# Three product kinds of a by-token matmul: interleaved per weight row block, or grouped by kind

## The chip, the core and the metric

The kernel runs on one core of a Trainium2 chip. The metric is the device time of one execution in microseconds (us), the median of three timed runs: 1079.44 us for the kernel before (1079.11 to 1079.62). TensorE is called PE below, VectorE DVE, ScalarE ACT, GpSimd POOL, and the engine that issues the weight transfers SP.

## The reference

Two layers of an encoder trunk over 256 tokens of width 1024, in fp32. Each layer is a gated feed-forward block, a mixer and a second feed-forward block, each added to its input; a norm follows the last layer. Cut to the places that matter here:

```python
x = x + 0.5 * swiglu(rmsnorm(x, ffn1_norm[l]), ffn1_w_gate[l], ffn1_w_up[l], ffn1_w_down[l])
h = rmsnorm(x, mix_norm[l])
z = h @ w_in            # [pool 512 | q 512 | f 512 | i 512 | out-gate 512 | branch gates 2 x 1024]
pool_out = causal_pool_mixer(u_pool, pool_w, pool_scale)
hgrn_out = hgrn2(q, f, i) * silu(og)
g = sigmoid(gates)
merged = g[:, :, 0] * (pool_out @ w_pool_proj) + g[:, :, 1] * (hgrn_out @ w_hgrn_proj)
x = x + merged @ w_out
x = x + 0.5 * swiglu(rmsnorm(x, ffn2_norm[l]), ffn2_w_gate[l], ffn2_w_up[l], ffn2_w_down[l])
```

## The kernel before

**Products in parts.** Weights and activations are fp32, the products use fp32r operands. Each operand is cut into a high part (rounded to fp32r) and a low part (what the rounding left), and a product is the sum of high x high, high x low and low x high. Weights come from HBM in chunks of 128 x 2048 values by SP's queue, in the order of the list `stream`. `parts` (lines 127 to 129) makes a chunk's two parts in two halves of 1024 columns each: ACT casts `raw` to `hi` (L128), DVE subtracts `raw - hi` into `lo` (L129). There are four `raw` buffers and three each of `hi` and `lo`; `weights(key)` prepares three chunks ahead.

**Two shapes of product.** Where the output is wanted with features on partitions, the weights are stationary and the tokens stream: `wide_run` (L182) multiplies 128 x 128 of `hi` with the high and low parts of 256 tokens side by side (512 columns, L186), for all tiles of a chunk, and then 128 x 128 of `lo` with the high parts (256 columns, L188). `mm_wide` (L176) does the same with the two kinds alternating (L179, L180). Where the output is wanted with tokens on partitions, `by_tokens` (L208) has 128 tokens of x stationary, and 512 columns of the weights stream. It is used for v, the out-gate and the four gate blocks of each layer's mixer (x is `xs`), for the two projections `pp` and `hp` of each half b of the 1024 columns, and in `last` for the down projection of the last feed-forward block. A chunk holds four blocks of 128 weight rows, so one call of `by_tokens` on a chunk makes, for each half h of the tokens, four times three products into one PSUM tile (two chunks together in the last group of `last`).

**The end of a mixer, called the merge below.** For b = 0 and 1: `pp` products, times a sigmoid on DVE (L751); `hp` products, times another on DVE (L757) into z, and the sum of both (L758). z is 128 tokens x 512 columns; it has two buffers, and there are four z per layer, named (b, h) below. `turned` (L705) turns each by four PE transposes (L709) into one of two PSUM tiles `gps`, from which ACT takes the high part (L247) and DVE the low part (L248) into the tiles `mhl` (named b4 to b7 in the trace of the first layer). Then the output projection `wo` (chunks 60 to 62 of the first layer) multiplies these by `mm_wide`: its first product needs b4 with the tokens of both halves, so z(0,0) and z(0,1) turned.

**What sets the order.** Tile code is recorded in the order of the source; a scheduler that estimates times then fixes one order of instructions per engine and the buffers. Work inside `urgent()` (z, the transposes, `residual`) gets a higher priority. On the chip each engine goes through its own list in that order, and waits on semaphores where it needs another's result.

Of the kernel before, what the change touches and what calls it, by code (L numbers as in the profile page):

```python
# [68 lines left out]
def _body(ctx, tc, a, out):  # L69
# [9 lines left out]
    mm = nc.tensor.matmul  # L79
# [128 lines left out]
    def by_tokens(pss, ws, x, ks, nk):  # L208


        for h in range(2):
            th = slice(h * P, h * P + P)
            for i, k in enumerate(ks):
                wh, wl = ws[i // 4]
                sl = slice(i % 4 * 512, i % 4 * 512 + 512)
                mm(pss[h], x(k)[:, 0, th], wh[:, sl], start=k == 0, stop=False)  # L216
                mm(pss[h], x(k)[:, 0, th], wl[:, sl], start=False, stop=False)  # L217
                mm(pss[h], x(k)[:, 1, th], wh[:, sl], start=False, stop=k == nk - 1)  # L218

    def urgent():  # L220
        return tc.high_priority(offset=URGENT)
# [136 lines left out]
    def last(hidden):  # L358

        ss = const.tile([P, 2, 2], F32, name="ss")  # L360
        r = const.tile([P, 2, 2], F32, name="ssr")
        for b in range(2):
            cols = slice(512 * b, 512 * b + 512)
            pss = token_tiles()
            for group in ((0,), (1,), (2,), (3,), (4, 5)):
                ws = [weights(("dt", b, i)) for i in group]
                by_tokens(pss, ws, hidden, range(4 * group[0], min(4 * group[-1] + 4, KF)), KF)
            for h in range(2):
                x = fin[1 + h][:, cols]
                with urgent():  # L370
                    nc.vector.scalar_tensor_tensor(
                        out=x, in0=pss[h], scalar=0.5, in1=x, op0=ALU.mult, op1=ALU.add)
                    junk = tmp.tile([P, 512], F32, tag="s1", name="junk")
                    nc.scalar.activation(junk, x, AF.Square, scale=D ** -0.5, accum_out=ss[:, h, b:b + 1])
                    if b == 0:
                        nc.vector.tensor_scalar_add(out=r[:, h, 0:1], in0=ss[:, h, 0:1], scalar1=EPS)
                        nc.gpsimd.tensor_mul(out=x, in0=x, in1=fin[0][:, cols])
                        continue
                    rh = r[:, h, 1:2]
                    tt(out=rh, in0=ss[:, h, 1:2], in1=r[:, h, 0:1], op=ALU.add)  # L380
                    nc.gpsimd.tensor_tensor(out=rh, in0=rh, in1=cst[:, C_M05:C_M05 + 1], op=ALU.pow)
                    first = fin[1 + h][:, 0:512]
                    nc.scalar.mul(out=first, in_=first, mul=rh)
                    nc.scalar.dma_start(out=out[:, h, 0:512], in_=first)
                    nc.vector.scalar_tensor_tensor(
                        out=x, in0=x, scalar=rh, in1=fin[0][:, cols], op0=ALU.mult, op1=ALU.mult)
                    nc.sync.dma_start(out=out[:, h, cols], in_=x)
# [92 lines left out]
    def mixer(l, sq, gain):  # L480
# [31 lines left out]
        for i in range(2):  # L512
            by_tokens(vps, [weights(("v", l, i))], xs, range(4 * i, 4 * i + 4), KD)
# [146 lines left out]
        def token_step(name, i):  # L660
            if i == 0:
                blocks_[name] = token_tiles()
            by_tokens(blocks_[name], [weights((name, l, i))], xs, range(4 * i, 4 * i + 4), KD)
            return blocks_[name]
# [178 lines left out]
```

## Time and profile before

| | us |
|---|---|
| median of three runs | 1079.44 |
| the profiled execution, its own time | 1079.82 |
| its span, first to last instruction | 1078.0 |
| PE busy in the span | 1064.3 (99%) |
| DVE busy | 813.9 (75%) |
| ACT busy | 566.7 (53%) |
| POOL busy | 129.9 (12%) |
| mean granted TensorE clock, of full | 0.998 |

The profiled execution took 1.8 us more than its span, and 0.4 us more than the median. PE's busy time is a sum of modelled spans that overlap; how long PE really needs for a product is read from the distance of one start to the next. PEld is PE's load of the stationary operand, beside the products. In the views below, an idle time in brackets stands with the engine and tile whose result ended it; an instruction of ACT or DVE that has no bracket followed the one before it directly.

### The profile page before, as it was taken

Reading aid. Unit: us, or ns where it says so; the run is one execution under the profiler, and the core shown is the slowest. Engines: PE = TensorE matmul, PEld = TensorE weight load, DVE = VectorE, ACT = ScalarE, POOL = GpSimd, SP = SyncE. Lnnn points to the kernel's source line nnn. Section 1 sums busy time; section 2 is a strip of 40 time slices with the busy share of each in tenths; the row PEclk is TensorE's granted clock in tenths of the full one; section 3 lists DMA queues with packets and bytes.
Section 4 is the critical chain, followed back from the end, with each engine's and each line's share of the span. In section 5 each row is a group of like instructions: output and inputs, shape, how many; then the busy total and the mean of one; then the engine's idle time right before and its main releaser. Section 6 shows DMA issues by size and latency. Waiting matters only on the chain.

```text
span 1078.0 us, 15379 instructions
## 1 busy us (share of the span) xinstructions
PE 1064.3 (99%) x5890; PEld 918.3 (85%) x5890; DVE 813.9 (75%) x1261; ACT 566.7 (53%) x953; POOL 129.9 (12%) x130
## 2 busy tenths in 40 slices
PE   9999999999999999999999999999999999999997
PEld 7888888887888888888888888888878788888885
DVE  7887767789667987777777776777995779777642
ACT  7675544544435655554455555446345456555532
POOL 2000001038100200000100000111560011000010
PEclk9999999999999999999999999999999999999999
DMA  9755456553543655546755544674445446555441
GB/s 332 273 185 174 135 185 232 189 193 116 205 156 121 237 190 194 171 139 189 249 200 192 193 157 140 210 265 169 152 130 183 161 172 234 188 174 191 171 137 39
DMA packets 32506, 197.34 MB, mean 183 GB/s; under 512 B 3616, under 2 KB 4512, under 8 KB 14000
## 3 DMA queue, kind: packets, MB, share of 16 engines
q1 hardware_dynamic: 31824, 195.50, 52.9%
q8 instruction: 46, 0.75, 0.3%
q10 hardware_dynamic: 576, 0.79, 0.2%
q14 instruction: 28, 0.23, 0.1%
q0 software_dynamic: 32, 0.07, 0.0%
HBM read 195.29 MB, written 1.05 MB: 182 GB/s over the span
## 4 chain that ended last, share of the span: by engine, by line
PE 90%; DVE 4%; POOL 3%; issue 2%; DMA 1%; ACT 0%; POOLq 0%; SPq 0%; DVEq 0%
PE ps L186 43%; PE ps L188 22%; PE ps L218 6%; PE ps L217 6%; PE ps L216 6%; PE ps L179 4%; PE ps L180 2%; DVE lo L129 2%; POOL win L636 1%; POOL b L557 1%; POOL b L556 1%; PE gps L590 1%; DMA xg<-in_x 0%; DVE m L555 0%; PE gps L693 0%
## 5 line engine op out<-in xcount | busy, mean ns | idle before, releaser
L129 DVE TENSOR_TENSOR lo<-raw,hi 128x1024 fp32r<-128x1024 f32 (+4 forms) x406 | 461.6, 1172 | 167.8 <-ACT hi L128 128.1
L128 ACT CAST hi<-raw 128x1024 fp32r<-128x1024 f32 (+4 forms) x406 | 373.7, 967 | 276.9 <-PE ps L186 97.7
L186 PE MATMUL ps<-xs__93,hi 128*128 128x512 f32 x1504 | 363.6, 393 | 0.0
L186 PEld LDWEIGHTS ps<-xs__93,hi 128*128 128x128 f32 x1504 | 275.0, 188 | 54.1
L188 PEld LDWEIGHTS ps<-xs__93,lo 128*128 128x128 f32 x1504 | 188.7, 188 | 8.2
L188 PE MATMUL ps<-xs__93,lo 128*128 128x256 f32 x1504 | 191.1, 278 | 0.0
L186 PE MATMUL ps<-b,hi 128*128 128x512 f32 x528 | 128.7, 391 | 0.0
L186 PEld LDWEIGHTS ps<-b,hi 128*128 128x128 f32 x528 | 95.7, 188 | 17.8
L273 POOL TENSOR_TENSOR acc<-acc,sq 128x256 f32<-128x256 f32 x42 | 37.4, 890 | 606.6 <-issue 392.2
L247 ACT CAST b<-h 128x256 fp32r<-128x256 f32 x88 | 35.6, 407 | 131.1 <-DVE h L427 131.1
L217 PE MATMUL ps<-lo,xs__93 128*128 128x512 f32 x192 | 76.9, 400 | 0.0
L216 PE MATMUL ps<-hi,xs__93 128*128 128x512 f32 x192 | 76.7, 399 | 0.0
L218 PE MATMUL ps<-hi,xs__93 128*128 128x512 f32 x192 | 76.2, 397 | 0.0
L202 DVE TENSOR_TENSOR z<-ps,zl 128x256 f32<-128x256 f32 x200 | 75.2, 416 | 0.1
L188 PEld LDWEIGHTS ps<-b,lo 128*128 128x128 f32 x528 | 68.2, 188 | 4.0
L188 PE MATMUL ps<-b,lo 128*128 128x256 f32 x528 | 69.2, 278 | 0.0
L201 ACT COPY zl<-ps 128x256 f32<-128x256 f32 x200 | 63.9, 365 | 6.9 <-PE ps L188 4.2
L423 DVE TENSOR_TENSOR z<-z,rb 128x512 f32<-128x512 f32 x88 | 60.0, 685 | 0.0
L217 PE MATMUL ps<-lo,b 128*128 128x512 f32 x152 | 59.9, 394 | 0.0
L216 PE MATMUL ps<-hi,b 128*128 128x512 f32 x152 | 59.8, 397 | 0.0
L218 PE MATMUL ps<-hi,b 128*128 128x512 f32 x152 | 59.5, 396 | 0.0
L179 PE MATMUL ps<-b,hi 128*128 128x512 f32 x128 | 45.5, 398 | 0.7 <-DVE b L248 0.7
(135 smaller groups left out, 960.6 us busy)
## 6 DMA issues: line engine op xcount, KB each, us to landing
raw<-in_gu SPq DMA_DIRECT2D x82, 1024.0 KB, 4.9
raw<-in_dn SPq DMA_DIRECT2D x48, 704.0 KB, 4.1
raw<-in_wt SPq DMA_DIRECT2D x24, 1024.0 KB, 4.9
raw<-in_wi SPq DMA_DIRECT2D x12, 1024.0 KB, 4.9
raw<-in_dt SPq DMA_DIRECT2D x10, 1024.0 KB, 5.0
raw<-in_wo SPq DMA_DIRECT2D x8, 1024.0 KB, 4.9
raw<-in_gu SPq DMA_DIRECT2D x8, 512.0 KB, 8.4
raw<-in_pp SPq DMA_DIRECT2D x4, 1024.0 KB, 4.9
```

The costliest lines, as they stand in the source:

```text
L128: a = nc.scalar.copy(out=hi[:, sl], in_=raw[:, sl])
L129: return a, tt(out=lo[:, sl], in0=raw[:, sl], in1=hi[:, sl].bitcast(F32), op=ALU.subtract)
L179: mm(ps, wh[:, sl], x, start=start, stop=False)
L186: mm(ps, wh[:, c:c + P], x, start=start, stop=False)
L188: mm(ps[:, 0], wl[:, c:c + P], x[:, 0], start=False, stop=stop)
L201: nc.scalar.copy(out=zl[:, g], in_=pss[g][:, 1])
L202: tt(out=z[:, g], in0=pss[g][:, 0], in1=zl[:, g], op=ALU.add)
L216: mm(pss[h], x(k)[:, 0, th], wh[:, sl], start=k == 0, stop=False)
L217: mm(pss[h], x(k)[:, 0, th], wl[:, sl], start=False, stop=False)
L218: mm(pss[h], x(k)[:, 1, th], wh[:, sl], start=False, stop=k == nk - 1)
L273: return nc.gpsimd.tensor_add(out=self.acc, in0=self.acc, in1=sq)
L423: tt(out=z, in0=z, in1=bc(rb, 2), op=ALU.mult)
```

## The change

Only `by_tokens` is changed. The loop over the three kinds of product now stands outside the loop over the weight row blocks: for a half of the tokens, first all products of x's high part with the weights' high part, then all of x's high part with the weights' low part, then all of x's low part with the weights' high part. Number, shapes, operands and PSUM tile of the products are the same, as are first and last product of each accumulation over a whole width of x. All three kinds now stand on line 216, and every later line number is one less than before.

```diff
         for h in range(2):
             th = slice(h * P, h * P + P)
-            for i, k in enumerate(ks):
-                wh, wl = ws[i // 4]
-                sl = slice(i % 4 * 512, i % 4 * 512 + 512)
-                mm(pss[h], x(k)[:, 0, th], wh[:, sl], start=k == 0, stop=False)
-                mm(pss[h], x(k)[:, 0, th], wl[:, sl], start=False, stop=False)
-                mm(pss[h], x(k)[:, 1, th], wh[:, sl], start=False, stop=k == nk - 1)
+            for part, low in ((0, False), (0, True), (1, False)):
+                for i, k in enumerate(ks):
+                    sl = slice(i % 4 * 512, i % 4 * 512 + 512)
+                    mm(pss[h], x(k)[:, part, th], ws[i // 4][low][:, sl], start=k == 0 and not (part or low),
+                       stop=k == nk - 1 and part == 1)
```

PE, the first out-gate chunk of the first layer (`hi46`, `lo46`; ps_2435 is the half h = 0 of the tokens, ps_2436 h = 1), before:

```order
L216 MATMUL ps_2435<-hi46_2300,xs__93 128x512
L217 MATMUL ps_2435<-lo46_2301,xs__93 128x512
L218 MATMUL ps_2435<-hi46_2300,xs__93 128x512
L216 MATMUL ps_2435<-hi46_2300,xs__93 128x512
L217 MATMUL ps_2435<-lo46_2301,xs__93 128x512
L218 MATMUL ps_2435<-hi46_2300,xs__93 128x512
```

The same place now:

```order
L216 MATMUL ps_2435<-hi46_2300,xs__93 128x512 x4
L216 MATMUL ps_2435<-lo46_2301,xs__93 128x512 x4
L216 MATMUL ps_2435<-hi46_2300,xs__93 128x512 x4
L216 MATMUL ps_2436<-hi46_2300,xs__93 128x512 x4
L216 MATMUL ps_2436<-lo46_2301,xs__93 128x512 x4
L216 MATMUL ps_2436<-hi46_2300,xs__93 128x512
```

What alternated product by product now comes in blocks of four, and the first product with the low part is the fifth and no longer the second.

PE, the merge of the first layer, from the middle of the last `hp` products (ps_3098 is b = 1, h = 1; z_3049 is z(0,1), z_3131 is z(1,0), z_3143 is z(1,1)) to the first `wo` products, before:

```order
L709 MATMUL gps_3052<-cst_91,z_3049 128x128 x4
L216 MATMUL ps_3098<-hi59_3006,b3_2800 128x512
L217 MATMUL ps_3098<-lo59_3007,b3_2800 128x512
L218 MATMUL ps_3098<-hi59_3006,b3_2800 128x512
L216 MATMUL ps_3098<-hi59_3006,b3_2800 128x512
L217 MATMUL ps_3098<-lo59_3007,b3_2800 128x512
L218 MATMUL ps_3098<-hi59_3006,b3_2800 128x512
L179 MATMUL ps_3172<-b4_2963,hi60_3064 128x512
L180 MATMUL ps_3172<-b4_2963,lo60_3065 128x256
```

and further down on PE before, after eight pairs of `wo` products:

```order
L179 MATMUL ps_3274<-b4_2963,hi62_3157 128x512
L709 MATMUL gps_3134<-cst_91,z_3131 128x128 x4
L180 MATMUL ps_3274<-b4_2963,lo62_3158 128x256
L179 MATMUL ps_3274<-b4_2963,hi62_3157 128x512
L180 MATMUL ps_3274<-b4_2963,lo62_3158 128x256
L709 MATMUL gps_3146<-cst_91,z_3143 128x128 x4
L179 MATMUL ps_3172<-b5_2964,hi60_3064 128x512
```

PE there now:

```order
L216 MATMUL ps_3098<-hi59_3006,b2_2799 128x512 x2
L216 MATMUL ps_3098<-hi59_3006,b3_2800 128x512 x2
L708 MATMUL gps_3052<-cst_91,z_3049 128x128 x4
L708 MATMUL gps_3134<-cst_91,z_3131 128x128 x4
L179 MATMUL ps_3172<-b4_2963,hi60_3064 128x512
L180 MATMUL ps_3172<-b4_2963,lo60_3065 128x256
```

The transposes of z(0,1) have moved from within the last `hp` products to behind them, and those of z(1,0) from within the `wo` products to ahead of them. Those of z(1,1) (gps_3146) stay behind ten pairs of `wo` products on b4.

DVE at the same place (`lo62` is the third `wo` chunk; b4_2963<-gps_3052 is the low part of z(0,1) for the first `wo` products), before:

```order
L757 TENSOR_TENSOR z_3131<-ps_3097,b10_1985 128x512
L248 TENSOR_TENSOR b5_2964<-gps_3040,b5_2964 128x2x128
L248 TENSOR_TENSOR b4_2963<-gps_3052,b4_2963 128x2x128
L757 TENSOR_TENSOR z_3143<-ps_3098,b11_1986 128x512
L758 TENSOR_TENSOR z_3131<-z_3131,b0_2961 128x512
L129 TENSOR_TENSOR lo62_3158<-raw62_3156,hi62_3157 128x1024
L758 TENSOR_TENSOR z_3143<-z_3143,b1_2962 128x512
L129 TENSOR_TENSOR lo62_3158<-raw62_3156,hi62_3157 128x1024
L248 TENSOR_TENSOR b5_2964<-gps_3052,b5_2964 128x2x128
```

DVE there now:

```order
L247 TENSOR_TENSOR b5_2964<-gps_3040,b5_2964 128x2x128
L756 TENSOR_TENSOR z_3131<-ps_3097,b10_1985 128x512
L756 TENSOR_TENSOR z_3143<-ps_3098,b11_1986 128x512
L757 TENSOR_TENSOR z_3131<-z_3131,b0_2961 128x512
L129 TENSOR_TENSOR lo62_3158<-raw62_3156,hi62_3157 128x1024
L757 TENSOR_TENSOR z_3143<-z_3143,b1_2962 128x512
L129 TENSOR_TENSOR lo62_3158<-raw62_3156,hi62_3157 128x1024
L247 TENSOR_TENSOR b4_2963<-gps_3052,b4_2963 128x2x128
```

The low part b4 of z(0,1) has moved from ahead of z(1,1)'s first step to behind both sums and both halves of `lo62`. ACT's list changes in the same way there (the high part of z(0,1) moves behind the cast of chunk 62); the same changes stand in the second layer. Elsewhere the lists of DVE and ACT differ only in one swap in `last`, and those of POOL and SP not at all; the small products between the gate blocks stand at the same place, give or take two products.

## Rows read from the trace of the kernel before

**Rows 1.** The page: busy time (us, share of the span), granted clock by slice, chain.

```profile
PE 1064.3 (99%) x5890; PEld 918.3 (85%) x5890; DVE 813.9 (75%) x1261; ACT 566.7 (53%) x953; POOL 129.9 (12%) x130
...
PEclk9999999999999999999999999999999999999999
...
PE 90%; DVE 4%; POOL 3%; issue 2%; DMA 1%; ACT 0%; POOLq 0%; SPq 0%; DVEq 0%
```

**Rows 2.** Waits of PE, whole span: who, for whom, total us, times, longest.

```profile
PE gps L590 <- DVE m L555: 3.6, 2, 1.8
...
PE ps L179 <- DVE b L248: 0.7, 2, 0.4
PE gps L709 <- DVE b L248: 0.6, 2, 0.3
```

**Rows 3.** Groups of PE by line and shape: count, busy us, mean ns, idle before.

```profile
L216 PE MATMUL ps<-hi,xs__93 128*128 128x512 f32 x192 | 76.7, 399 | 0.0
...
L216 PE MATMUL ps<-hi,b 128*128 128x512 f32 x152 | 59.8, 397 | 0.0
```

**Rows 4.** The chain in order of time: start us, us until the next, what.

```profile
47.25 3.66 PE ps L186 x16
...
1036.16 0.23 PE ps L216
...
1041.76 0.23 PE ps L216
```

**Rows 5.** Instructions in order of time (start us, us, engine line): the second v chunk.

```profile
199.60 2.00 ACT L128 CAST hi<-raw 128x1024 fp32r<-128x1024 f32 x2 [6.38 <-PE ps L186]
...
201.85 2.36 DVE L129 TENSOR_TENSOR lo<-raw,hi 128x1024 fp32r<-128x1024 f32 x2 [2.36 <-ACT hi L128]
...
204.91 0.39 PE L216 MATMUL ps<-hi,xs__93 128*128 128x512 f32 x1
```

**Rows 6.** Instructions of PE in order of time: the merge of the first layer.

```profile
329.12 0.60 PE L709 MATMUL gps<-cst,z 128*128 128x128 f32 x4
...
329.79 0.40 PE L217 MATMUL ps<-lo,b 128*128 128x512 f32 x1
...
330.72 0.40 PE L218 MATMUL ps<-hi,b 128*128 128x512 f32 x1
331.48 0.50 PE L179 MATMUL ps<-b,hi 128*128 128x512 f32 x1 [0.36 <-DVE b L248]
...
335.40 0.28 PE L180 MATMUL ps<-b,lo 128*128 128x256 f32 x1
335.98 0.63 PE L709 MATMUL gps<-cst,z 128*128 128x128 f32 x4 [0.30 <-DVE b L248]
```

**Rows 7.** Instructions of ACT, then DVE, in order of time: the same merge.

```profile
329.75 0.37 ACT L247 CAST b<-gps 128x256 fp32r<-128x256 f32 x1 [1.45 <-PE gps L709]
...
331.35 0.68 DVE L757 TENSOR_TENSOR z<-ps,b 128x512 f32<-128x512 f32 x1
331.95 0.68 DVE L758 TENSOR_TENSOR z<-z,b 128x512 f32<-128x512 f32 x1
332.55 1.22 DVE L129 TENSOR_TENSOR lo<-raw,hi 128x1024 fp32r<-128x1024 f32 x1
333.68 0.69 DVE L758 TENSOR_TENSOR z<-z,b 128x512 f32<-128x512 f32 x1
334.28 1.22 DVE L129 TENSOR_TENSOR lo<-raw,hi 128x1024 fp32r<-128x1024 f32 x1
335.42 0.75 DVE L248 TENSOR_TENSOR b<-gps,b 128x256 fp32r<-128x256 f32 x2
```

**Rows 8.** A stretch after the last product: busy PE to POOL, clock, DMA share, GB/s.

```profile
1074.00:1078.00 4.00, 0.00 (x0) 0.00 (x0) 0.26 (x1) 0.23 (x1) 0.00 (x0) 0.55 0.35 131
```

**Rows 9.** Groups of PE, as in rows 3: two kinds of 128-column products.

```profile
L574 PE MATMUL gps<-qx,b 128*128 128x128 f32 x32 | 4.2, 274 | 0.0
L228 PE MATMUL wps<-warm 128*128 128x128 f32 x18 | 4.2, 430 | 1.1 <-DVE warm L225 1.1
```

## The prediction, made before the changed kernel was run

> **What bounds the kernel now.** I read the page first: PE is busy in 99% of the span, the clock stands at full in all forty slices, and the chain that ended last runs through PE for 90% of its length [rows 1]. So every us that PE gains or waits is a us of the result, wherever it lies. Next the waits of PE: the reader is to see how short the list is. PE waits twice for DVE's L555 (3.6 us together), twice for DVE's L248 before L179 and twice before L709, once in each layer [rows 2]. No product of lines 216 to 218 is in that list, and their groups have no idle time before them [rows 3]. An order that lets the low parts come later can therefore save no wait: there is none. Two things remain that a new order can change: the pace of the products, and the few waits that exist. Of these the merge, at the end of each mixer, is the one place where the lists of PE, ACT and DVE come out differently.
>
> **Waits for the weights' parts: nothing.** With the products grouped, the first low part is wanted at the fifth product of a chunk and not at the second, which is harmless. But the second half of `hi` is wanted at the third product and no longer at the seventh, four products of 0.23 us earlier, and the second half of `lo` at the seventh instead of the eighth. The chunk that is made last before its use is v's second: its `hi` is cast by 201.60 and its `lo` done by 204.21, and its first product starts at 204.91 [rows 5]. The cover is 3.3 us for `hi`, and over 2 us for the second half of `lo`, against a need that moves by 0.9 and 0.2 us. If that cover were gone, a chunk would cost up to 0.9 us. Buffers come free with a chunk's last product, as before.
>
> **Pace: nothing, with an end at -4.6 us.** There are 3 x (192 + 152) = 1032 products of the three lines [rows 3]. Between 1036.16 and 1041.76 stand 24 of them, so one takes 5.60 / 24 = 0.2333 us. A run of L186, with the same number of columns, takes 3.66 / 16 = 0.2288 us [rows 4]. The products of L186 go through one weight tile block after block; those of lines 216 to 218 change between two weight tiles with each product. They also have the roles of the operands exchanged. If the alternation makes the difference, the grouped order gains up to 1032 x 0.0045 = 4.6 us (three quarters of it, 3.5 us, if each change of kind, after four products, still pays). If the roles make it, the order gains nothing. No row shows x stationary without the alternation, so both ends stand. On the other side, no dense run of such products is slower than 0.2333, and I see nothing that the new order adds, so that end is zero too. I take zero: the only rows with x stationary have this pace, at v and gates as in `last`, whatever tile is stationary.
>
> The Trainium skill (TensorE: Matmul & The Clock Gate, section "Back-to-back issue gap") has the gap of products in a row depend on the number of columns alone, N / 2.4 + 2.5 ns, 216 ns for 512 columns. By it the pace term would be zero whichever order is chosen. The trace agrees in part only: 0.2288 and 0.2333 us for the same 512 columns are more than the page's figure, and they differ from each other.
>
> **The merge: +3.3 us per layer.** The schedule puts the transposes of z(0,1) behind all `hp` products, those of z(1,0) behind them, both before the first `wo` product, and on DVE the low part b4 of z(0,1) behind both sums of b = 1 and both halves of `lo62`. I follow the first layer with the durations before.
>
> Step 1: PE passes the last `hp` product earlier, because one group of transposes no longer stands ahead of it. A group costs 0.44: from 329.12 to 329.79 lie the group and one product, 0.67 - 0.23 [rows 6]. The last product starts at 330.72 - 0.44 = 330.28, and the transposes of z(0,1) at 330.28 + 0.23 = 330.51.
>
> Step 2: z(1,1) needs the buffer which those transposes read (z has two buffers). A result of transposes starting at 329.12 was taken up at 329.75, 0.63 later [rows 6, 7]. So DVE's L757 for z(1,1) starts at 330.51 + 0.63 = 331.14, about where it starts now (331.35).
>
> Step 3: DVE goes on as now. From L757 to L758 are 0.60, and L758 takes 0.68 [rows 7]: z(1,0) is complete at 331.14 + 0.60 + 0.68 = 332.42. Its transposes, next on PE, can't start before; PE has been free since 330.95, a new wait of 1.5 us.
>
> Step 4: from the start of L757 to that of L248 DVE needs now 335.42 - 331.35 = 4.07 us, with two sums and two halves of `lo62` between [rows 7]. The same five instructions stand ahead of L248 for b4 in the new list, so it starts at 331.14 + 4.07 = 335.21 and, with 0.42 for one of the two in its row, ends at 335.63. The first `wo` product wants b4 and starts at about 335.68; PE, done with z(1,0) at 332.9, waits another 2.8 us. Now it starts at 331.48 [rows 6], so the stage is 4.20 late.
>
> Step 5: what it saves later. Before, two groups of transposes stand within the following `wo` products, 2 x 0.44, and the second waits: 335.98 - 335.40 = 0.58, less the 0.12 of L180 itself, 0.46 [rows 6]. Now one group stands there, and nothing is late for it: z(1,1) is summed by about 334.1, PE comes past at 339. Saved: 0.44 + 0.46 = 0.90.
>
> Per layer 4.20 - 0.90 = 3.3 us. It isn't given back: behind the merge PE runs without a wait for ACT or DVE [rows 2], and it is those two that have time to spare. The waits of PE in rows 2 show the same place twice, once per layer, and the lists change alike in both: 2 x 3.3 = 6.6 us. Bounds: if ACT or DVE were ready earlier than step 2 has them, z(1,1) couldn't start earlier (PE sets it); if DVE comes to step 2 late, by the 0.3 us or so that it has to spare there, the term grows by as much. I take 2.8 to 3.7 per layer.
>
> The two waits for L555 stay: the small products ahead of which they lie keep their place among the gate products, and what they wait for starts on DVE and POOL.
>
> **Sum.** 1079.82 for the profiled execution, +0 for the parts, +0 for the pace, +6.6 for the merge: 1086.4. It lies 0.4 above the median of the runs, so the forecast against that median is **1086.0 us**, 0.6% slower.
>
> **Rivals.**
> *The pace rises to that of the wide runs.* For it: the one obvious difference between the sequences is the alternation. Against: the roles differ too, and the pace of lines 216 to 218 is the same where the schedule mixes the products of two chunks. Price -4.6 us against +6.6: 1081.4, within 0.2% of before, so not slower; with three quarters, 1082.5. It decides the sign of the verdict from about 0.2291 us per product.
> *The clock falls in the new pause.* PE would have from 330.5 to 335.7 only eight transposes. For it: after the last product of the program the granted clock goes from 1.00 to a mean of 0.55 within 1074 to 1078, so it does fall in a pause, to the lower of its levels [rows 8]. Against: all slices of before are at full, with waits of 1.8 us in them. A stretch like that of the start, where 18 products take 4.2 us that 32 of their kind take later [rows 9], would lose 4.2 x (1 - 18/32) = 1.8 us each time: 1087.8 for one layer, 1089.6 for both.
> The Trainium skill (same page, "What's actually happening") says that activity holds the upper level and that an idle PE goes back to 1.2 GHz; by it this rival is possible, and the trace agrees for the end of the program.
> *The change does nothing that can be measured*: DVE and ACT have more slack at the merge than my steps give them, and the pace stays: 1079.4 to 1081.
>
> **How the numbers follow.** Forecast as it stands 55%, the faster pace 20%, the clock 15% (in two thirds of it in one layer only), nothing measurable 10%. The range reaches from the faster pace to the clock's fall in one layer with the upper bound of the merge: 1081.0 to 1089.0; what lies outside is most of the last rival and the clock's fall in both layers, some 15%. A measurement can tell about 0.2% (2.2 us) from no change. Slower by more than that, over 1081.6: forecast, clock, and the half of the faster pace in which it is partial, 79%. Within: the other half of it and most of the last rival, 17%. Faster: 4%.
>
> **What would show it.** In the list of PE's waits: two new entries per layer, at the transposes of z(1,0) (about 1.5 us, for DVE's sum) and at the first `wo` product (about 2.8 us, for DVE's low part); before it was 0.4 and 0.3. On DVE, `lo62` twice ahead of b4's low part. In the chain: 24 products of line 216 in 5.60 us, or 5.49 if the pace rises. In the clock by slice: full at both merges. Wrong would be: products of line 216 with idle time before them, no wait at the merge, or a pace between 0.2333 and the end that I gave.

## The result, and the profile after

| | before | changed |
|---|---|---|
| median | 1079.45 us | 1091.22 us |
| lowest to highest, four runs each | 1079.11 to 1079.62 | 1089.90 to 1091.91 |
| the profiled execution, its own time | 1079.82 | 1090.58 |
| its span | 1078.0 | 1088.8 |
| mean granted clock, of full | 0.998 | 0.993 |

The changed kernel is slower: the ratio is 1.0107, 95% interval 1.0095 to 1.0120. The forecast was 1086.0 with a range up to 1089.0, so the direction was right and the size was not. What follows finds 10.8 us between the two profiled executions: 6.6 at the merge, as forecast, 3.7 from the clock, which fell at both merges, and 0.5 at the start. The medians are 11.8 apart. The four executions of the changed kernel differ in their mean granted clock: 1089.90 us at 0.995, 1090.58 (the profiled one) at 0.993, 1091.86 and 1091.91 at 0.992. So the last us is most likely clock too, which isn't shown, since only one execution has a trace.

The page of the changed kernel first (busy time; granted clock by slice; the chain by engine), answering to [rows 1]:

```profile
PE 1067.7 (98%) x5890; PEld 921.8 (85%) x5890; DVE 812.7 (75%) x1261; ACT 566.3 (52%) x953; POOL 130.7 (12%) x130
...
PEclk9999999999999999999999999999999999999999
...
PE 91%; POOL 3%; DVE 2%; issue 2%; DMA 1%; SPq 0%; ACT 0%; POOLq 0%; DVEq 0%
```

It reads almost as before. PE still carries the end, and the clock is "9" in every slice: a slice is 27 us long, and a nine only says 90% or more, so a fall of a few us can't be seen in this row. The list of what PE waits for does show a difference (who, for whom, total us, times, longest), answering to [rows 2]:

```profile
PE ps L179 <- DVE b L247: 5.0, 2, 2.5
PE gps L589 <- DVE m L554: 3.5, 2, 1.8
PE gps L708 <- DVE z L757: 2.9, 2, 1.5
PE ps L179 <- ACT hi L128: 1.2, 2, 1.0
```

The two waits at the level products (now L589) are unchanged. New are 1.5 us per layer before the transposes of z(1,0), for DVE's sum, and 2.5 before the first `wo` product, for DVE's low part. The last row, a wait for the first weights, was 0.2 in the profile of before. There is still no wait at line 216. Runs of its products in the chain, with one of L186 ahead (start us, us until the next, what):

```profile
47.74 3.66 PE ps L186 x16
...
268.04 5.60 PE ps L216 x24
...
1020.33 57.41 PE ps L216 x246
```

24 grouped products take 5.60 us, to the digit what 24 alternating ones took [rows 4], and 246 of them in the last block 57.41, which is 0.2334 each. The first row gives the start: the same run of L186 began at 47.25 [rows 4] and now begins at 47.74. These 0.49 us were lost in the first 17 us, while the first weights arrive, and they differ from execution to execution: `one_mixed` below has 0.7 us of that wait in its profile and the median of before.

Now PE at the merge of the first layer, answering to [rows 6]:

```profile
331.00 0.60 PE L708 MATMUL gps<-cst,z 128*128 128x128 f32 x4
333.07 0.63 PE L708 MATMUL gps<-cst,z 128*128 128x128 f32 x4 [1.47 <-DVE z L757]
336.19 0.51 PE L179 MATMUL ps<-b,hi 128*128 128x512 f32 x1 [2.49 <-DVE b L247]
...
337.25 0.63 PE L179 MATMUL ps<-b,hi 128*128 128x512 f32 x1
...
337.89 0.63 PE L179 MATMUL ps<-b,hi 128*128 128x512 f32 x1
...
340.64 0.39 PE L179 MATMUL ps<-b,hi 128*128 128x512 f32 x1
...
340.99 0.40 PE L179 MATMUL ps<-b,hi 128*128 128x512 f32 x1
...
341.34 0.60 PE L708 MATMUL gps<-cst,z 128*128 128x128 f32 x4
```

and DVE, answering to [rows 7]:

```profile
331.63 0.69 DVE L756 TENSOR_TENSOR z<-ps,b 128x512 f32<-128x512 f32 x1 [0.36 <-PE gps L708]
332.24 0.68 DVE L757 TENSOR_TENSOR z<-z,b 128x512 f32<-128x512 f32 x1
332.84 1.22 DVE L129 TENSOR_TENSOR lo<-raw,hi 128x1024 fp32r<-128x1024 f32 x1
333.98 0.69 DVE L757 TENSOR_TENSOR z<-z,b 128x512 f32<-128x512 f32 x1
334.58 1.22 DVE L129 TENSOR_TENSOR lo<-raw,hi 128x1024 fp32r<-128x1024 f32 x1
335.71 1.61 DVE L247 TENSOR_TENSOR b<-gps,b 128x256 fp32r<-128x256 f32 x4
```

The reader is to see two things. The first `wo` product starts at 336.19 instead of 331.48, 4.71 later; without the 0.49 of the start that is 4.22, where the forecast has 4.20. And behind the pause a pair of L179 and L180 takes 0.64 us (337.25 to 337.89), while three us later it takes 0.35 (340.64 to 340.99). The stretches of both merges, in windows (start:end, length, busy PE, PEld, DVE, ACT, POOL with their counts, granted clock, DMA share, GB/s), first layer and then second:

```profile
335.00:336.00 1.00, 0.00 (x0) 0.00 (x0) 1.00 (x2) 0.00 (x0) 0.00 (x0) 1.00 0.00 0
336.00:337.00 1.00, 0.81 (x3) 0.71 (x4) 0.89 (x4) 0.70 (x2) 0.00 (x0) 0.84 0.91 115
337.00:340.00 3.00, 3.00 (x11) 2.58 (x10) 0.33 (x1) 0.00 (x0) 0.00 (x0) 0.50 0.73 306
```

```profile
870.00:872.00 2.00, 0.70 (x2) 0.60 (x3) 1.90 (x4) 0.70 (x2) 0.00 (x0) 0.50 0.56 131
...
874.00:876.00 2.00, 2.00 (x9) 1.71 (x8) 0.00 (x0) 0.00 (x0) 0.00 (x0) 0.50 0.59 242
```

A granted clock of 0.50 is the lower of the two levels, 1.2 GHz. In the first layer it comes when PE is already at work again, in the second while PE still stands (it resumes at 871.30).

**The account.** For the second layer the same places are wanted in both kernels: first `wo` product and transposes of z(1,1), before and then after.

```profile
861.79 0.50 PE L179 MATMUL ps<-b,hi 128*128 128x512 f32 x1 [0.37 <-DVE b L248]
...
866.28 0.63 PE L709 MATMUL gps<-cst,z 128*128 128x128 f32 x4 [0.27 <-DVE b L248]
```

```profile
871.30 0.80 PE L179 MATMUL ps<-b,hi 128*128 128x512 f32 x1 [2.49 <-DVE b L247]
...
877.03 0.60 PE L708 MATMUL gps<-cst,z 128*128 128x128 f32 x4
```

From the first `wo` product to the transposes of z(1,1) before took 335.98 - 331.48 = 4.50 us, of which 0.90 were the transposes of z(1,0) and a wait (step 5 of the forecast), so 3.60 of products. After takes 341.34 - 336.19 = 5.15: the lower clock cost 1.55. In the second layer it is 4.49 - 0.90 = 3.59 before and 5.73 after, 2.14. By then the first layer has left the kernel 341.34 - 335.98 = 5.36 late, and the first `wo` product of the second layer comes 871.30 - 861.79 = 9.51 late, 4.15 more.

| | us |
|---|---|
| start | 0.5 |
| merge, first layer: 4.22 - 0.90 | 3.3 |
| lower clock, first layer | 1.6 |
| merge, second layer: 4.15 - 0.90 | 3.3 |
| lower clock, second layer | 2.1 |
| sum | 10.8 |

The two profiled executions differ by 1090.58 - 1079.82 = 10.76.

### The profile page after: what moved, and what is told of

Its sections match the earlier page's. It is cut to its first block, busy times and chain, and to the rows that moved or that the text cites. A ratio compares the mean times of both kernels' runs of the same rounds, so it can differ in the third digit from the quotient of the medians.

```text
span 1088.8 us, 15377 instructions
## 1 busy us (share of the span) xinstructions
PE 1067.7 (98%) x5890; PEld 921.8 (85%) x5890; DVE 812.7 (75%) x1261; ACT 566.3 (52%) x953; POOL 130.7 (12%) x130
## 4 chain that ended last, share of the span: by engine, by line
PE 91%; POOL 3%; DVE 2%; issue 2%; DMA 1%; SPq 0%; ACT 0%; POOLq 0%; DVEq 0%
PE ps L186 42%; PE ps L188 21%; PE ps L216 19%; PE ps L179 5%; PE ps L180 2%; DMA raw<-in_gu 1%; DVE lo L129 1%; POOL win L635 1%; POOL b L556 1%; POOL b L555 1%; PE gps L589 1%; PE gps L708 0%; DVE m L554 0%; PE gps L692 0%; POOL pd L639 0%
## 5 line engine op out<-in xcount | busy, mean ns | idle before, releaser
L186 PE MATMUL ps<-xs__93,hi 128*128 128x512 f32 x1504 | 363.5, 393 | 0.0
L186 PEld LDWEIGHTS ps<-xs__93,hi 128*128 128x128 f32 x1504 | 275.0, 188 | 54.0
L186 PE MATMUL ps<-b,hi 128*128 128x512 f32 x528 | 128.7, 391 | 0.0
L186 PEld LDWEIGHTS ps<-b,hi 128*128 128x128 f32 x528 | 95.7, 188 | 17.8
L216 PE MATMUL ps<-hi,xs__93 128*128 128x512 f32 x384 | 101.4, 398 | 0.0
L216 PEld LDWEIGHTS ps<-hi,xs__93 128*128 128x128 f32 x384 | 70.9, 188 | 15.8
L216 PE MATMUL ps<-hi,b 128*128 128x512 f32 x304 | 77.9, 395 | 0.0
L216 PEld LDWEIGHTS ps<-hi,b 128*128 128x128 f32 x304 | 56.7, 187 | 13.7
L216 PE MATMUL ps<-lo,xs__93 128*128 128x512 f32 x192 | 55.5, 400 | 0.0
L179 PE MATMUL ps<-b,hi 128*128 128x512 f32 x128 | 49.0, 421 | 5.0 <-DVE b L247 5.0
L216 PEld LDWEIGHTS ps<-lo,xs__93 128*128 128x128 f32 x192 | 35.8, 188 | 8.0
```

Of the source, the lines that this page charges most:

```text
L179: mm(ps, wh[:, sl], x, start=start, stop=False)
L186: mm(ps, wh[:, c:c + P], x, start=start, stop=False)
L216: mm(pss[h], x(k)[:, part, th], ws[i // 4][low][:, sl], start=k == 0 and not (part or low), stop=k == nk - 1 and part == 1)
```

## The experiments

The theory is that grouping costs nothing where it stands: the whole loss is the order that the schedule chooses at the merge, and the clock that falls in the pause which this order makes. The rivals: the grouped products cost by themselves; the fall has another cause than the standstill. Each run was timed beside runs of the kernel before on the same chip (1079.5 to 1079.7).

### All grouped but one call, and the reverse

Comparing the programs, the lists of all engines at the merge turned out to hang on one call: the `hp` products of b = 0, 24 per layer. Both runs use `by_tokens` with a choice:

```diff
+            order = [(p, i, k) for p in kinds for i, k in enumerate(ks)]
+            if mixed:
+                order = [(p, i, k) for i, k in enumerate(ks) for p in kinds]
...
-            by_tokens(pss, [weights(("hp", l, b))], lambda k: part(yhl, k), range(4), 4)
+            by_tokens(pss, [weights(("hp", l, b))], lambda k: part(yhl, k), range(4), 4, b == 0)
```

In `one_mixed` only that call alternates. In `one_grouped` the sense is turned round, and only that call is grouped.

> All by-token products grouped by kind as in the changed kernel, but in one call: the hp products of the first half of the columns (24 products per layer) alternate as before. The lists of PE, ACT and DVE at the merge are then those of the kernel before. Theory A (grouping costs nothing by itself; the whole loss is the order that the schedule takes at the merge, 6.6 us, and the clock that falls in the pause there, 3.6 us and more): 1079.4, within 1 us, and no wait of PE at the merge over 0.4 us. Rival B (the grouped order costs by itself, by pace or clock, wherever it stands): 984 of 1032 products are still grouped, so some 1090.

Measured: 1079.70 us, ratio 1.0001 (0.9992 to 1.0010).

> The reverse: every by-token call alternates the kinds as in the kernel before, and only the hp products of the first half of the columns (24 per layer, 48 of 1032) are grouped. The lists at the merge are then those of the changed kernel. Theory A: the whole loss, 1091 (1089.5 to 1092), with PE's two waits per layer of 1.5 and 2.5 us and the clock at its lower level behind them. Rival B: 48 of 1032 products cost a twentieth of the loss, 1080.

Measured: 1090.26 us (1088.83 to 1091.79), ratio 1.0099 (1.0085 to 1.0113). PE's waits, `one_mixed` and then `one_grouped`:

```profile
PE ps L179 <- DVE b L250: 0.7, 2, 0.4
```

```profile
PE ps L179 <- DVE b L250: 5.0, 2, 2.5
...
PE gps L711 <- DVE z L760: 2.9, 2, 1.5
```

984 grouped products cost nothing that can be measured (-0.9 to +1.1 us); 48 grouped ones carry the whole loss. That also settles the pace: an effect of 4.6 us is excluded. What these 48 change is an order. Alternating, all products of that call stand ahead of the last six `pp` products of b = 1 in PE's list; grouped, nine of the twelve for the second half of the tokens stand behind the last `pp` product. So z(0,1) comes later on DVE. Its first step there, in the profiles of before and after:

```profile
323.28 0.69 DVE L757 TENSOR_TENSOR z<-ps,b 128x512 f32<-128x512 f32 x1 [2.11 <-PE ps L218]
```

```profile
326.79 0.68 DVE L756 TENSOR_TENSOR z<-ps,b 128x512 f32<-128x512 f32 x1
```

Before, this step waited for PE; now it follows DVE's own step before it, so the new order on DVE has a share in the 3.5 us. That everything behind it in the merge follows from this one step is argued and not shown: no run moves the nine products alone, and why the schedule ranks them behind the others was not tried.

### Ten products in the second pause

The changed kernel with work for PE between the transposes of z(1,0) and the first `wo` product. It goes into a PSUM tile that the first `wo` product overwrites; no other instruction moves.

```diff
+            with tc.issue_after(turns[-5].ins):
+                for _ in range(10 if i0 == 0 else 0):
+                    mm(pss[0], ws[0][0][:, 0:P], part(phl, 0), start=True, stop=True)
```

> The changed kernel with ten products more per layer, whose result is overwritten: PE does them between the transposes of z(1,0) and the first wo product, where it waits 2.5 us; ten take 10 x 0.233 = 2.3 us. Nothing else moves. Theory A (the clock falls because PE stands still there): the first wo product starts when it does now, the clock stays at full, and what the slow products behind the pause cost (1.6 us in the first layer, 2.0 in the second) goes: 1087.6, with 1087.0 to 1088.2. Rival C (the first pause of 1.5 us is enough for the fall, or the fall comes from something else than the standstill): 1091 as now, or up to 1092 where the ten products run at the lower level and hold up the next.

Measured: 1087.09 us (1085.99 to 1087.21), ratio 1.0066 (1.0054 to 1.0079), 4.1 less than the changed kernel. PE at the merge of the first layer (L771 are the ten; the last row is the transposes of z(1,1)), and then the windows of both merges:

```profile
333.16 0.63 PE L710 MATMUL gps<-cst,z 128*128 128x128 f32 x4 [1.47 <-DVE z L759]
333.54 2.54 PE L771 MATMUL ps<-b,hi 128*128 128x512 f32 x10
336.27 0.51 PE L179 MATMUL ps<-b,hi 128*128 128x512 f32 x1 [0.20 <-DVE b L247]
...
339.89 0.60 PE L710 MATMUL gps<-cst,z 128*128 128x128 f32 x4
```

```profile
337.00:341.00 4.00, 4.00 (x26) 3.56 (x25) 0.48 (x3) 0.37 (x1) 0.00 (x0) 1.00 0.64 246
...
870.00:872.00 2.00, 2.00 (x12) 1.73 (x13) 0.90 (x3) 0.55 (x2) 0.00 (x0) 1.00 0.78 184
```

The first `wo` product starts at 336.27, where it started in the changed kernel (336.19), and the clock is at full behind it. The useless work makes the kernel faster, and the forecast's merge term stands nearly alone: 1087.1 - 1079.7 = 7.4 by the medians, with an interval of 5.8 to 8.5 from the ratio, where the forecast has 6.6. With the clock at full this trace also shows the merge by itself. Its start and its transposes of z(1,1) in the second layer:

```profile
47.83 3.66 PE ps L186 x16
```

```profile
873.50 0.60 PE L710 MATMUL gps<-cst,z 128*128 128x128 f32 x4
```

The transposes of z(1,1) come 339.89 - 335.98 = 3.91 us later than before, of which 47.83 - 47.25 = 0.58 are the start: 3.33 for the first layer. In the second they come 873.50 - 866.28 = 7.22 later, 3.31 more. That is the forecast's 3.3 per layer, measured without the lower clock.

### Six products in the first pause

The same with six products between the transposes of z(0,1) and those of z(1,0), so that the pause of 2.5 us stays (`turns[-9]`, `range(6 ...)`).

> The changed kernel with six products more per layer, whose result is overwritten, between the transposes of z(0,1) and those of z(1,0): they take 6 x 0.233 = 1.4 us of the 1.5 us that PE waits there, and the second pause, of 2.5 us, stays. Nothing else moves. Theory A1 (the second pause alone brings the clock down): as the changed kernel, 1090 to 1091.5, with wo products at the lower level behind the pause. Theory A2 (it takes both pauses, so little work in the whole stretch of five us): as with ten products in the second pause, 1087.0, clock at full.

Measured: 1088.72 us (1087.71 to 1090.09), ratio 1.0085 (1.0072 to 1.0099). Windows behind both merges:

```profile
337.00:341.00 4.00, 4.00 (x16) 3.43 (x15) 0.41 (x2) 0.00 (x0) 0.00 (x0) 0.57 0.61 240
...
872.00:875.00 3.00, 3.00 (x19) 2.59 (x18) 0.54 (x2) 0.08 (x1) 0.00 (x0) 1.00 1.00 330
```

Neither expectation is met: the median lies between the two. In the profiled execution the clock fell in the first layer and not in the second, behind the same pause of 2.5 us in both. So this pause alone brings the clock down in some cases; together with the first one, of 1.5 us, it did so in both layers of the profiled executions of the changed kernel and of `one_grouped`.

### The low part of chunk 62 behind b4

The changed kernel with the two halves of `lo62` put behind the low part of z(0,1) on DVE, where the schedule had them ahead.

```diff
-            ws = [weights(("wo", l, i), 3 if i < 3 else 2) for i in (i0, i0 + 1)]
+            with tc.issue_after(lows[2].ins) if i0 == 0 else ExitStack():
+                ws = [weights(("wo", l, i), 3 if i < 3 else 2) for i in (i0, i0 + 1)]
```

> The changed kernel with one step moved on DVE: both halves of lo62 behind the low part b4 of z(0,1) instead of ahead of it; PE and ACT keep the lists of the changed kernel. Theory A: b4 is done 2.3 us earlier, so the first wo product comes 2.3 us earlier in each layer (PE's wait before it 0.2 to 0.5 instead of 2.5), and the shorter pause keeps the clock up: 1091.2 - 2 x 2.3 - 3.6 = 1083.0. Rival C (the fall has another cause, or the pause that is left is enough for it): 1086.6. Rival D (the wait is not for that DVE step): 1091.

Measured: 1082.48 us (1081.74 to 1085.07), ratio 1.0029 (1.0018 to 1.0041). PE and then DVE at the first merge:

```profile
332.76 0.63 PE L710 MATMUL gps<-cst,z 128*128 128x128 f32 x4 [1.47 <-DVE z L759]
333.70 0.50 PE L179 MATMUL ps<-b,hi 128*128 128x512 f32 x1 [0.32 <-DVE b L247]
```

```profile
333.23 0.42 DVE L247 TENSOR_TENSOR b<-gps,b 128x256 fp32r<-128x256 f32 x1
333.57 2.35 DVE L129 TENSOR_TENSOR lo<-raw,hi 128x1024 fp32r<-128x1024 f32 x2
```

Two DVE instructions put behind a third give back 8.7 us of the changed kernel's 11.8. Between the profiled executions it is 1090.58 - 1082.57 = 8.0: PE's waits for b4 in both layers together fall from 5.0 us to 0.9, which is 4.1, and the 3.7 of the clock go with them, since the granted clock is full at both merges. That confirms which DVE step PE waits for. The highest of the six runs, 1085.07, has a mean granted clock of 0.996 where the others have 0.998 or 0.999; a fall at one merge would explain it, but no row shows it.

### The larger wait that both kernels have

PE's longest waits before were the two of 1.8 us at the products of level 16 [rows 2]. Since a version faster than both kernels would have to save there, three runs moved these products later on PE, in the kernel before (alternating), by eleven, five and eight products of a gate block. The diff, cut to the step itself, is that of eight; five has `(0, 0)`, and eleven has `(0, 2)` without the last two lines:

```diff
+                if held and (h, i) == (0, 1):
+                    with urgent(), tc.issue_after(last.ins):
+                        held.pop()()
+                    with tc.issue_after(kept[-1].ins):
+                        prepare(at[0] + 1)
```

> The kernel before, its by-token products alternating, with one step moved on PE: the small products of level 16 (128 columns, for which PE waits 1.8 us in each layer) eleven products of a gate block later, 2.6 us; the levels behind them follow by some eight products. This is the one larger wait of PE that both kernels have. If nothing else becomes late: 1079.6 - 2 x 1.8 = 1076.0, and no wait of PE for DVE's m left. Rival (the later steps, the small products of the next levels and the tokens' outputs, come late by as much and make PE wait there): 1079.6.

Measured: 1086.80 us, ratio 1.0068 (1.0056 to 1.0081), slower than both values expected. The wait for L555 is gone, and one for the predicated copies of level 16 (now L570) is there instead, with the clock at its lower level behind it:

```profile
270.47 2.04 PE L595 MATMUL gps<-m 128*128 128x128 f32 x8 [3.42 <-DVE at__2287 L570]
```

```profile
272.00:276.00 4.00, 4.00 (x12) 3.23 (x12) 4.00 (x4) 0.00 (x0) 3.78 (x4) 0.50 0.45 188
```

The schedule had answered the move by putting both halves of the low part of chunk 51 ahead of those copies on DVE. The next two keep DVE's order but for one or two steps that stand a few places off.

> The kernel before with the small products of level 16 five products later on PE (1.17 us) and, unlike in the run with eleven, the order of everything else on DVE kept: only one half of the low part of chunk 51 stands one place earlier. Theory E (moving the step was right, and in the run with eleven it was the DVE order that came with it, low parts ahead of a step that PE waits for, that made the new wait): PE waits 0.6 instead of 1.8 us before level 16, and for nothing new: 1079.6 - 2 x 1.17 = 1077.3. Rival F (any delay of a level comes back at the next one): 1079.6 or slower.

Measured: 1080.34 us, ratio 1.0005 (0.9996 to 1.0013).

> As the run with five, but eight products later (1.87 us), which is the whole wait; on DVE the second half of the low part of chunk 51 stands one place earlier and one small step ahead of the predicated copies of level 32, and on PE the next two levels stand two products later. Theory E: 1079.6 - 2 x 1.8 = 1076.0. Rival F: 1079.6 or slower; and in between where the low part of chunk 51 ahead of level 32's copies holds up PE again.

Measured: 1080.64 us, ratio 1.0011 (1.0002 to 1.0020). PE's waits in that stage of the run with five, first layer:

```profile
259.34 1.13 PE L597 MATMUL gps<-m 128*128 128x128 f32 x8 [0.63 <-DVE m L562]
...
266.00 1.13 PE L597 MATMUL gps<-m 128*128 128x128 f32 x8 [0.40 <-DVE at__2287 L572]
...
276.99 1.13 PE L597 MATMUL gps<-m 128*128 128x128 f32 x8 [0.56 <-DVE b L662]
```

Of 1.8 us, 0.63 are left in the old place, and 0.40 + 0.56 have come up at the next two levels: 1.6 in all. With eight products the old wait is gone, and 0.65 at the next level and 1.17 at the small products behind it stand in its place, 1.8 in all. My theory E falls, F holds: in these runs the levels follow one another on DVE and set how soon PE can be through with them. Without fewer or shorter DVE steps there, a place later on PE only moves the wait. No version that beats both kernels came out.

## Why the prediction was right at the merge and wrong on the clock

- **Weights' parts: nothing.** Right; line 216 has no idle time before it.
- **Pace: nothing.** Right: 5.60 us for 24 products as before, 0.2334 in a run of 246, and `one_mixed` with 984 grouped products is within 1 us of the kernel before. The rival of the faster pace is out: what makes 0.2333 and 0.2288 differ is not the change of tile from product to product. What it is stays open. The formula that the prediction cites beside this term from the Trainium skill (TensorE: Matmul & The Clock Gate, section "Back-to-back issue gap") stands there for one product by itself; for a stream in which each product has its own weight load, as here (5890 of each), that section lets both set the spacing. So it was no support for taking zero, which rests on the rows alone.
- **The merge: +3.3 per layer.** Right, step by step; `filled` shows 3.33 and 3.31. With the 0.49 of the start added, the forecast has the transposes of z(0,1) at 331.00, z(1,1)'s first step on DVE at 331.63, b4's low part at 335.70 and the first `wo` product at 336.17; the trace has 331.00, 331.63, 335.71 and 336.19. The waits are 1.47 and 2.49 against 1.5 and 2.8, where the forecast let the second one begin some 0.3 too early. The saving of 0.9 is also there: no wait stands before the transposes of z(1,1) any more.
- **The clock: the step that failed.** The sum has no term for it: it lets PE run at full clock behind the new pause, and the runs show 3.7 us lost there. The rival "the clock falls in the new pause" was the truth, in both layers, and its price was about right (1.8 us per layer forecast, 1.6 and 2.1 measured; 1089.6 for both against 1091.2). That is in part luck: the price was taken from the start of the kernel, and PE's products ran slow for longer in the second layer than in the first. The rival was given 15%, and two thirds of that for one layer only, and so the range ended at 1089.0. The rows did not bear out so small a chance. "All slices of before are at full" [rows 1] says nothing on this: the slices of the changed kernel are all nines too. And the waits of 1.8 us in which the clock held [rows 2] were taken as evidence for a stretch of five us with eight transposes in it; the only place of before with a longer pause is behind the last product, and there the clock did fall [rows 8], though not at once:

```profile
1071.00:1074.00 3.00, 0.16 (x1) 0.00 (x0) 1.34 (x3) 1.21 (x3) 0.56 (x1) 1.00 0.45 168
```

  It stayed full for 2.8 us without a product and fell after that. The new stretch, pauses of 1.5 and 2.8 us with a few transposes around them, was like neither, so the rows left the rival open.
- By the rule of the Trainium skill named beside that rival (TensorE: Matmul & The Clock Gate, section "What's actually happening"), an idle PE goes back to 1.2 GHz. The trace agrees: 0.50 at 337 to 340 and at 870 to 876, in the first layer only once PE was at work again; full in `filled`, where PE had work in the pause.
- **The start, 0.5 us,** is no term of the change: the profiled execution of before had its first weights that much sooner. In a sum against one profiled execution it is an error of this size.
- **The rival of nothing measurable** ("ACT and DVE have more slack than my steps give them") is out: the steps came to 0.02 us of the trace.

The list of waits would have shown the forecast right; only the windows around the pause show what came on top.

## What to carry to other kernels

When a change makes PE wait, ask how long the waits are in which the clock is known to hold in this kernel; a pause longer than all of them has to be priced with the lower clock behind it as well, here 3.7 us on top of a delay of 6.6. The loss from a change in the order of products can hang on one call out of many, by what a scheduler makes of it on another engine: compare the engines' lists call by call, and leave alone the call that tips them. And where PE waits for a chain of steps on another engine, moving its own instruction later does not shorten the chain.

## What the hardware showed that was not expected

- In the profiled executions of the changed kernel, `one_grouped` and `later_level` the clock fell in or just behind each pause of 2.5 or 3.4 us; at the waits of 1.8 us and less, in all profiled executions, it did not fall. The same pause of 2.5 us brought it down at one merge of an execution and not at the other (`fill_first`), and in the first layer of the changed kernel the fall came after PE had resumed (full in 335 to 336, where PE was idle, 0.50 from 337, where it was busy throughout). The times of the kernels with such a pause scatter, 1089.9 to 1091.9 for the changed kernel against 1079.1 to 1079.6 before, and the slower executions have the lower mean clock: in `one_grouped` 1088.8 and 1089.4 us at 0.995, 1091.1 and 1091.8 at 0.992.
- Work that is thrown away, ten products per layer in a pause, made the kernel 4.1 us faster.
- Products with x stationary kept 0.2333 us in both orders, 0.0045 more than those with the weights stationary and the same 512 columns.
